# A decoder layer on one core: attention scores and outputs as three float32r products of rounded parts and remainders, with 32 work slots in place of 36

## The chip, the cores and the metric

The kernel runs on one core of one Trainium2 chip. The metric is the device time of one execution in microseconds; the median of the runs is compared. TensorE (PE in the profile) multiplies matrices, with its weight loads listed apart as PEld; VectorE is DVE, ScalarE is ACT, GpSimd is POOL, and SyncE (SP) issues most of the loads. Matrix products are summed in PSUM, in banks of 128 partitions by 512 float32 values. Everything else lives in SBUF.

## The reference

One decoder layer on 512 positions of width 1024, all in float32. It has two halves, a mixer and a feed-forward network (FFN). The mixer projects the normalised input u to queries, keys, values, output gates, forget and input gates (four heads of width 256) and to a convolution group. Queries and keys pass a causal convolution of four taps and SiLU. Per head, with chunks of 128 positions, the reference computes

```python
scores = jnp.einsum("bhtd,bhsd->bhts", q_, k_) * jnp.exp(dmat - m_t[..., None])
num = (w_inter[..., None] * jnp.einsum("bhtd,bhde->bhte", q_, C)
       + jnp.einsum("bhts,bhse->bhte", scores, v_))
den = w_inter * jnp.einsum("bhtd,bhd->bht", q_, n) + jnp.sum(scores, axis=-1)
h = num / jnp.maximum(jnp.abs(den), jnp.exp(-m_t))[..., None]
```

The kernel does this without the chunks' carried state, as one causal attention over all 512 positions: scores times a decay matrix E, then times the values, with two columns of ones behind the values that give the sum of the scores. The heads' outputs are normalised, gated, put beside the convolution group's output (31 taps, layer norm, SiLU), and multiplied by an output matrix. The FFN has an up projection to 2 x 2816, a convolution of three taps, a gated product, and a down projection.

## The kernel before, in words

**Products.** float32 operands are mostly multiplied as three products of float32r values. A tile x is split into a rounded part, hi = x copied by ACT into a float32r tile, and a remainder, lo = x - hi, by POOL or DVE. `mm3` (line 207) then adds hi·hi, hi·lo and lo·hi into one bank. The weights are split by `w_split` (line 185): ACT rounds (line 191), POOL subtracts (line 192). They come through `w_load` from two raw buffers of 1 MB, and a raw buffer is loaded again only when the last remainder has been taken from it. Two products of the attention are not done so: the scores (line 544) and the outputs (line 555) are plain float32 matmuls.

**Attention of one head** (`attention`, line 536) is a generator that is advanced in steps, between which other products are issued. Scores come in four tiles of 512, 384, 256 and 128 columns (causal, one per key chunk), each the sum of two products over the two halves of the head. VectorE multiplies each with its part of E (line 545). Then four output tiles, one per 128 positions, are sums of one to four products of a block of E with 258 columns of values (line 555): ten products a head. ACT takes them out of PSUM (lines 558 to 560), DVE, POOL and ACT work out a factor per position, TensorE transposes (line 586), and ACT and DVE split the result into hh and hl (lines 592, 593). Score, output and transposed tiles share the two banks of `atbank`.

**Order.** TensorE's and SP's instructions are issued in the order of the program. The order on ACT, DVE and POOL is a planner's: it simulates the program, takes the ready instruction of the highest priority (earliest in the program), and gives a tile its buffer when one is free; on the chip each of these engines then follows that order strictly. The taps of the 31-tap convolution (`conv_tile`, line 751: DVE at line 767, ACT and POOL at lines 761 and 763) have their priority lowered by LATER. Two parts (`in_order`) are fixed by hand.

**Loop over heads** (line 836). While head h is in attention, the projections of head h+1 run between its steps: four of q and k (`head_proj`, whose `conv4` at line 498 makes each q or k tile out of PSUM by one ACT, three DVE and one ACT instruction), then four tiles of values and gates (`make_vo`, line 483, where ACT copies the values out at line 494 and gates at line 495). The first steps of the last head's attention stand among the products of the output matrix (`mix_first`, bank mixa; later mixb).

**Buffers.** `slots` holds 36 tiles of 128x512 float32 that nearly everything uses: q and k, E, gates, head outputs, the 32 split tiles hy of heads and convolution group, mg, and in the FFN the split inputs of the down projection (`split_f`, line 1108). `vpool` has two buffers of 128x1032 float32: the values of a head, later a gain row and one pair of `split_f`. `cvs` has four tiles.

**End.** The down projection (line 1179 on, `product`) is one level of a seven-product scheme. It loads weights in groups through the two raw buffers and four `ring` buffers, all on SP's queue. Tiles s34 (11 pairs of slots) and a22 (6 pairs, two of them late) are read back from DRAM and split at lines 1228 and 1229. Ahead of the last product (p4, line 1280), SP's queue holds the load of row g2r into two slots (line 1275) and four loads of x1.

Of the kernel before, what the change touches and what calls it, by code (L numbers as in the profile page):

```python
# [10 lines left out]
F32 = mybir.dt.float32  # L11
F32R = mybir.dt.float32r
BF16 = mybir.dt.bfloat16
AF = mybir.ActivationFunctionType
ALU = mybir.AluOpType
PSUM = bass.MemoryType.PSUM

P = 128
D = 1024
T = 512  # L20
KT = D // P
NT = T // P
H = 4
# [3 lines left out]
CK = 31  # L27
LATER = 100000
EPS = 1e-6
SLOTS = 36  # L30
SIDES = 2
ADAS = 2
SIDE = 5
# [22 lines left out]
def decoder_layer(ctx, tc, w_glu0, x, c, adaT, vecs, w_glu, w_qko, w_v0, w_vo, w_out, w_up, w_down, out):  # L56
# [33 lines left out]
    def slot(name, dt=F32):  # L90
        return slots.tile([P, T], dt, tag="t", name=name)
# [325 lines left out]
        glu_ps[i // 2, i % 2] = ps  # L417
    cspool.__exit__(None, None, None)
    early_pool.__exit__(None, None, None)
    vpool = ctx.enter_context(tc.tile_pool(name="vpool", bufs=2))  # L420
    cvs = ctx.enter_context(tc.tile_pool(name="cvs", bufs=CVS))
    cvpool.append(ctx.enter_context(tc.tile_pool(name="cvpool", bufs=2, space=PSUM)))

# [27 lines left out]


    vs = [None] * H
    gz = const.tile([P, NT, 2 * H], F32, name="gz")
    GB = 2 * H

    def v_tile(h):
        va = vpool.tile([P, 2 * T + 8], F32, tag="vh", name=f"v{h}").rearrange("p (c n) -> p c n", c=NT)

        V.tensor_copy(va[:, :, DH:], ones[:, None, :2].to_broadcast([P, NT, 2]))  # L460
        vs[h] = [va[:, cc, :] for cc in range(NT)]

    def make_v0():

        n = DH + GB
        wv = []
        for q in range(0, KT, 4):
            r = raws.tile([P, 2048], F32, tag="raw", name=f"wv0_{q}")
            nc.sync.dma_start(r[:, : 4 * n], w_v0[q // 4])
            wv += [tuple(w[:, :n] for w in w_split(r[:, i * n : (i + 1) * n], f"wv0_{q + i}")) for i in range(4)]  # L470
        v_tile(0)
        banks = [mmbank(f"v0_{tt}") for tt in range(NT)]
        for tt, ps in enumerate(banks):
            ts = slice(tt * P, (tt + 1) * P)
            for k in range(KT):
                mm3(ps[:, :n], (u[k][0][:, ts], u[k][1][:, ts]), wv[k], k == 0, k == KT - 1)
            V.tensor_tensor(out=gz[:, tt, :], in0=ps[:, DH : DH + GB], in1=vcols("gate_b", 0, GB), op=ALU.add)
            S.activation(vs[0][tt][:, :DH], ps[:, :DH], AF.Copy)

    def part_of(two, tt):  # L480
        return two[tt // 2][:, (tt % 2) * DH : (tt % 2 + 1) * DH]
# [1 line left out]
    def make_vo(h):  # L483

        w = [z for q in range(2) for z in w_load(w_vo[h - 1, q], f"wvo{h}_{q}")]
        v_tile(h)
        gate = [slot(f"so{h}_{i}") for i in range(2)]
        heads[h][3].extend(gate)
        for tt in range(NT):
            ps = mmbank(f"vo{h}_{tt}")  # L490
            ts = slice(tt * P, (tt + 1) * P)
            for k in range(KT):
                mm3(ps, (u[k][0][:, ts], u[k][1][:, ts]), w[k], k == 0, k == KT - 1)
            S.activation(vs[h][tt][:, :DH], ps[:, :DH], AF.Copy)
            S.activation(part_of(gate, tt), ps[:, DH:], AF.Tanh, scale=0.5)
            yield

    def conv4(ps, i, name):

        t = slot(f"{name}c")  # L500
        w = lambda tap: vcol("qk_conv_w", tap * 16 + i)
        S.activation(t, ps, AF.Identity, bias=vcol("qk_conv_b", i), scale=w(3))
        for d in range(1, 4):
            last_e[0] = V.scalar_tensor_tensor(out=t[:, d:], in0=ps[:, : T - d], scalar=w(3 - d), in1=t[:, d:], op0=ALU.mult, op1=ALU.add)
        S.activation(t, t, AF.Silu)
        return t

    hy = [None] * (2 * KT)

# [26 lines left out]
    def attention(h):  # L536
# [3 lines left out]
        for cc in range(NT):  # L540
            n = NS[cc]
            sp = atbank(f"s{h}_{cc}")
            for d in range(2):
                PE.matmul(sp[:, :n], ks[d][:, cc * P : (cc + 1) * P], qs[d][:, cc * P :], start=d == 0, stop=d == 1)  # L544
            last_e[0] = V.scalar_tensor_tensor(out=E[h][cc], in0=sp[:, :n], scalar=DH**-0.5, in1=E[h][cc], op0=ALU.mult, op1=ALU.mult)
            if cc in ((0, 2, 3) if h == 0 else (1, 3)):
                yield
        ssq = small.tile([P, NT], F32, tag="ssq", name=f"ssq{h}")
# [2 lines left out]
        for tt in range(NT):  # L551
            o = atbank(f"o{h}_{tt}")
            for cc in range(tt + 1):
                a = (tt - cc) * P
                PE.matmul(o[:, : DH + 2], E[h][cc][:, a : a + P], vs[h][cc], start=cc == 0, stop=cc == tt)  # L555
            junk = small.tile([P, DH], BF16, tag="junk2", bufs=1, name=f"junko{h}_{tt}")
            hv = hn[tt // 2][:, (tt % 2) * DH : (tt % 2 + 1) * DH]
            S.activation(dm[:, tt : tt + 1], o[:, DH : DH + 1], AF.Abs)
# [56 lines left out]

    PLACE = [(0, 0), (1, 0), (2, 0), (1, 384)]

    def head_tiles(name, dt, three=None):
        three = three or [slots.tile([P, T], dt, tag="t", name=f"{name}{i}") for i in range(3)]
        return [three[s][:, a : a + n] for (s, a), n in zip(PLACE, NS)]  # L620

    E = [None] * H
# [59 lines left out]
    def send_rows(a, n, queue=nc.scalar):  # L682

        ps = mmbank(f"gT{a}") if a == KT else atbank(f"gT{a}")
        PE.transpose(ps[:n, :P], gains[:, a : a + n], ident)
        t = (side if a == 3 * KT else slot)(f"gTs{a}")[:, :P]
        V.tensor_copy(t[:n, :], ps[:n, :P])
        for i in range(n // KT):
            queue.dma_start(rows_d[a // KT + i].rearrange("(j p) -> j p", p=P), t[i * KT : (i + 1) * KT, :])
# [233 lines left out]
    for n in range(10, 2 * KT):  # L923
        mix_first(n)
        if n == 10:
            send_rows(0, KT)
    mg = [slot(f"mg{tt}") for tt in range(NT)]
    x1 = side_parts("x1_0") + side_parts("x1_1")
    x1 = [x1[2 * tt : 2 * tt + 2] for tt in range(NT)]
    wide1 = vpool.tile([P, 2 * T + 8], F32, tag="vh", name="g1r")  # L930
# [189 lines left out]
    for i in range(NF):  # L1120
# [29 lines left out]
        if i % 2:  # L1150
# [6 lines left out]
            if i == NF - 1:  # L1157
                ends = [adas.tile([P, D], F32R, tag="ada", name=f"f{q}{i}") for q in "xy"]
                home = [(z[:, :T], z[:, T:]) for z in ends]
            af.append(split_f(x_, f"fx{i}", i == 1, home[0]))  # L1160
            asum.append(split_f(y_, f"fy{i}", i == 1, home[1]))
            j = i // 2
            nc.scalar.dma_start(spill["s34"][:, j * T : (j + 1) * T], q_)
            nc.scalar.dma_start(spill["a22"][:, j * HT : (j + 1) * HT], r_[:, HT:])
# [200 lines left out]
```

## Time and profile before

| | |
|---|---|
| median of three runs | 771.68 us (770.37 to 772.17) |
| the profiled execution | 771.52 us, of which its span 769.8 us |
| TensorE busy | 758.5 us, 99% of the span |
| DVE, ACT, POOL busy | 573.7, 408.4, 522.7 us |
| TensorE clock granted | 0.998 of full |
| heads' stretch | 157.8 to about 345 us |

Times in the profile are microseconds from the start of the span. A row of a timeline has the start, the duration, the engine and line, and in brackets the idle time before it with what ended that. A row of groups has the number of instructions, their busy time, and the mean nanoseconds of one. The chain of waits follows the execution back from its end, so it lists for each stretch what set the pace. A row of waits has the total time, the number of times, and the longest. Matmul records overlap: their starts, not their durations, give the rate.

### The profile page before, as it was taken

To read this page: it belongs to the slowest core of one execution; us is meant where nothing else is said; L and a number is where in the kernel's file an instruction comes from. 1 tells how busy PE (TensorE), PEld (TensorE's weight loads), DVE (VectorE), ACT (ScalarE), POOL (GpSimd) and SP (SyncE) were. 2 spreads that over 40 slices of the span, in tenths; PEclk is the share of its full clock that TensorE was granted. 3 is DMA by queue.
4 is the path that set the end of the run, shared out by engine and by line. 5 is a ranking of instruction groups with operands and counts; after the bars stand their busy time and mean duration, and the time that the engine had idled before them with its cause. 6 is when DMAs were issued, how large, how long until landed. Compare 5 with 4: busy or idle time off the path is not lost.

```text
span 769.8 us, 10292 instructions
## 1 busy us (share of the span) xinstructions
PE 758.5 (99%) x3562; PEld 630.5 (82%) x3562; DVE 573.7 (75%) x831; ACT 408.4 (53%) x780; POOL 522.7 (68%) x432
## 2 busy tenths in 40 slices
PE   8999999999999999999999999999999999999996
PEld 6788898878788788788888998888888888888885
DVE  5669999979979696476949797675765677654548
ACT  7585438585665645573334554434445246566633
POOL 4789759795494871645611467886978786599943
PEclk9999999999999999999999999999999999999999
DMA  8973214311131250655953655856686584896273
GB/s 317 347 277 126 100 56 140 135 54 56 54 111 55 110 181 38 246 192 164 378 193 135 246 185 196 301 213 232 221 302 220 215 294 145 303 399 239 96 242 141
DMA packets 40137, 147.34 MB, mean 191 GB/s; under 512 B 3826, under 2 KB 5266, under 8 KB 30484
## 3 DMA queue, kind: packets, MB, share of 16 engines
q1 hardware_dynamic: 26372, 94.50, 34.1%
q10 hardware_dynamic: 13712, 52.18, 18.8%
q8 instruction: 28, 0.46, 0.2%
q14 instruction: 25, 0.20, 0.1%
HBM read 126.59 MB, written 20.07 MB: 191 GB/s over the span
## 4 chain that ended last, share of the span: by engine, by line
PE 91%; DMA 2%; DVE 2%; POOL 2%; issue 1%; ACT 1%; DVEq 0%; POOLq 0%; ACTq 0%
PE up L210 31%; PE qko L210 13%; PE dn L210 10%; PE vo L210 9%; PE glu L210 7%; PE mixa L210 6%; PE mixb L210 6%; PE s L544 2%; PE o L555 2%; PE glu L356 2%; PE v L210 1%; DMA p<-spill_t 1%; DMA wglu<-in_w_glu 1%; POOL wglu_0l L192 0%; PE cps L159 0%
## 5 line engine op out<-in xcount | busy, mean ns | idle before, releaser
L767 DVE SCALAR_TENSOR_TENSOR cv<-gt,cvw,cv 128x485 f32<-128x485 f32 (+23 forms) x200 | 137.1, 731 | 2.9 <-ACT cv L755 1.3
L763 POOL TENSOR_TENSOR cs<-cs,cs 128x510 f32<-128x510 f32 (+3 forms) x32 | 42.1, 1318 | 0.1
L210 PE MATMUL up<-u2l,wup_0h 128*128 128x512 f32 (+1 forms) x100 | 36.5, 365 | 0.1
L210 PE MATMUL up<-u2h,wup_0h 128*128 128x512 f32 (+1 forms) x100 | 36.5, 365 | 0.0
L210 PE MATMUL up<-u2h,wup_1024h 128*128 128x512 f32 (+1 forms) x100 | 36.4, 364 | 0.0
L210 PE MATMUL up<-u2h,wup_0l 128*128 128x512 f32 (+1 forms) x100 | 36.4, 364 | 0.0
L210 PE MATMUL up<-u2l,wup_512h 128*128 128x512 f32 (+1 forms) x100 | 36.4, 364 | 0.0
L210 PE MATMUL up<-u2h,wup_512h 128*128 128x512 f32 (+1 forms) x100 | 36.4, 364 | 0.0
L210 PE MATMUL up<-u2h,wup_1536h 128*128 128x512 f32 (+1 forms) x100 | 36.4, 364 | 0.0
L210 PE MATMUL up<-u2l,wup_1536h 128*128 128x512 f32 (+1 forms) x100 | 36.4, 364 | 0.0
L210 PE MATMUL up<-u2h,wup_1536l 128*128 128x512 f32 (+1 forms) x100 | 36.4, 364 | 0.0
L210 PE MATMUL up<-u2h,wup_512l 128*128 128x512 f32 (+1 forms) x100 | 36.4, 364 | 0.0
L210 PE MATMUL up<-u2h,wup_1024l 128*128 128x512 f32 (+1 forms) x100 | 36.4, 364 | 0.0
L210 PE MATMUL up<-u2l,wup_1024h 128*128 128x512 f32 (+1 forms) x100 | 36.3, 363 | 0.0
L176 DVE SCALAR_TENSOR_TENSOR junk<-ada,cb 128x1024 bf16<-128x1024 f32 x20 | 30.1, 1506 | 4.9 <-DMA ada<-in_adaT 4.8
L192 POOL TENSOR_TENSOR wup_0l<-wup,wup_0h 128x512 fp32r<-128x512 f32 x19 | 29.3, 1543 | 4.5 <-ACT wup_0h L191 4.5
L192 POOL TENSOR_TENSOR wup_1024l<-wup,wup_1024h 128x512 fp32r<-128x512 f32 x19 | 25.0, 1318 | 9.4 <-ACT wup_1024h L191 9.4
L192 POOL TENSOR_TENSOR wup_1536l<-wup,wup_1536h 128x512 fp32r<-128x512 f32 x19 | 27.6, 1455 | 4.7 <-ACT wup_1536h L191 4.4
L761 ACT ACTIVATE cs<-gt,cvw 128x511 f32<-128x511 f32 (+4 forms) x40 | 27.2, 712 | 6.3 <-POOL cs L763 3.8
L1099 DVE TENSOR_TENSOR b<-b 128x512 f32<-128x512 f32 x11 | 19.4, 1760 | 11.3 <-POOL b L1098 11.3
L1098 POOL TENSOR_TENSOR b<-b 128x512 f32<-128x512 f32 x11 | 14.2, 1291 | 17.3 <-DVE b L1097 17.3
L336 DVE SCALAR_TENSOR_TENSOR junk<-ada,cps 128x1024 bf16<-128x1024 f32 x16 | 19.5, 1219 | 8.3 <-ACT cb L411 4.6
(1097 smaller groups left out, 2738.5 us busy)
## 6 DMA issues: line engine op xcount, KB each, us to landing
wup<-in_w_up SPq DMA_DIRECT2D x22, 1024.0 KB, 6.0
b<-in_w_down ACTq DMA_DIRECT2D x11, 1024.0 KB, 5.1
spill_t<-b ACTq DMA_DIRECT2D x11, 1024.0 KB, 3.9
ada<-in_adaT ACTq DMA_DIRECT2D x20, 512.0 KB, 4.0
wqko<-in_w_qko SPq DMA_DIRECT2D x9, 1024.0 KB, 4.8
ada<-in_adaT SPq DMA_DIRECT2D x16, 512.0 KB, 7.2
wo<-in_w_out SPq DMA_DIRECT2D x8, 1024.0 KB, 4.8
wvo<-in_w_vo SPq DMA_DIRECT2D x6, 1024.0 KB, 4.8
```

The costliest lines, as they stand in the source:

```text
L176: t = V.scalar_tensor_tensor(out=junk, in0=r, scalar=1.0, in1=cb, op0=ALU.mult, op1=ALU.mult, accum_out=mod[:, i : i + 1])
L192: (eng or G).tensor_tensor(out=lo[:, :n], in0=src, in1=hi[:, :n].bitcast(F32), op=ALU.subtract)
L210: PE.matmul(ps, l, r, start=start and i == 0, stop=stop and i == 2, skip_group_check=again)
L336: V.scalar_tensor_tensor(out=junk, in0=first[k][:, i * D : (i + 1) * D], scalar=1.0, in1=cps, op0=ALU.mult, op1=ALU.mult, accum_out=part[: ...
L356: PE.matmul(ps, blk(wk, i)[a], u[k][b], start=k == 0 and p == 0, stop=k == KT - 1 and p == 1)
L544: PE.matmul(sp[:, :n], ks[d][:, cc * P : (cc + 1) * P], qs[d][:, cc * P :], start=d == 0, stop=d == 1)
L555: PE.matmul(o[:, : DH + 2], E[h][cc][:, a : a + P], vs[h][cc], start=cc == 0, stop=cc == tt)
L761: S.activation(t[:, d:], cvx[j][:, : T - d], AF.Copy, scale=w(CK - 1 - d))
L763: G.tensor_tensor(out=side[:, d:], in0=side[:, d:], in1=t[:, d:], op=ALU.add)
L767: tap = V.scalar_tensor_tensor(out=cp[:, d:], in0=cvx[j][:, : T - d], scalar=w(CK - 1 - d), in1=cp[:, d:], op0=ALU.mult, op1=ALU.add)
L1098: G.tensor_tensor(out=b12, in0=b22, in1=b12, op=ALU.subtract)
L1099: V.tensor_tensor(out=b22, in0=b22, in1=b11, op=ALU.subtract)
```

## The change

- The four q and k tiles of each head are split at the end of `conv4`: ACT rounds, POOL subtracts. Scores use `mm3`, for all four heads: three float32r products where one float32 product stood.
- For heads 0 to 2 (`SPLIT`), each tile of E, once multiplied with its scores, is split too (ACT, POOL), into six more slot tiles Eh and El a head, and the values are split as they leave PSUM (ACT, DVE). Outputs of these heads use `mm3`. Head 3 keeps plain outputs.
- Values take two buffers a head, and `vpool` has four. The columns of ones are written by ACT in place of DVE.
- `slots` shrinks from 36 to 32. The four tiles mg move to two `vpool` buffers, two small rows (gTs) move to `cvs`, and one more pair of `split_f` (i = 3) moves from slots to `vpool`.

```diff
-SLOTS = 36
+SLOTS = 32
...
-    vpool = ctx.enter_context(tc.tile_pool(name="vpool", bufs=2))
+    vpool = ctx.enter_context(tc.tile_pool(name="vpool", bufs=4))
...
+    SPLIT = range(H - 1)
...
     def v_tile(h):
-        va = vpool.tile([P, 2 * T + 8], F32, tag="vh", name=f"v{h}").rearrange("p (c n) -> p c n", c=NT)
-
-        V.tensor_copy(va[:, :, DH:], ones[:, None, :2].to_broadcast([P, NT, 2]))
-        vs[h] = [va[:, cc, :] for cc in range(NT)]
+        both = []
+        for i in range(2 if h in SPLIT else 1):
+            va = vpool.tile([P, 2 * T + 8], F32R if h in SPLIT else F32, tag="vh", name=f"v{h}_{i}").rearrange("p (c n) -> p c n", c=NT)
+            S.activation(va[:, :, DH:], ones[:, None, :2].to_broadcast([P, NT, 2]), AF.Copy, scale=1.0 - i)
+            both.append([va[:, cc, :] for cc in range(NT)])
+        vs[h] = both
+
+    def v_out(h, tt, ps):
+        hi = vs[h][0][tt][:, :DH]
+        S.activation(hi, ps[:, :DH], AF.Copy)
+        if h in SPLIT:
+            V.tensor_tensor(out=vs[h][1][tt][:, :DH], in0=ps[:, :DH], in1=hi.bitcast(F32), op=ALU.subtract)
...
-            S.activation(vs[0][tt][:, :DH], ps[:, :DH], AF.Copy)
+            v_out(0, tt, ps)
...
-            S.activation(vs[h][tt][:, :DH], ps[:, :DH], AF.Copy)
+            v_out(h, tt, ps)
...
         S.activation(t, t, AF.Silu)
-        return t
+        hi, lo = slot(f"{name}h", F32R), slot(f"{name}l", F32R)
+        S.activation(hi, t, AF.Copy)
+        G.tensor_tensor(out=lo, in0=t, in1=hi.bitcast(F32), op=ALU.subtract)
+        return hi, lo
...
-                PE.matmul(sp[:, :n], ks[d][:, cc * P : (cc + 1) * P], qs[d][:, cc * P :], start=d == 0, stop=d == 1)
+                mm3(sp[:, :n], [z[:, cc * P : (cc + 1) * P] for z in ks[d]], [z[:, cc * P :] for z in qs[d]], d == 0, d == 1)
             last_e[0] = V.scalar_tensor_tensor(out=E[h][cc], in0=sp[:, :n], scalar=DH**-0.5, in1=E[h][cc], op0=ALU.mult, op1=ALU.mult)
+            if h in SPLIT:
+                if cc == 0:
+                    Eh, El = head_tiles(f"Eh{h}_", F32R), head_tiles(f"El{h}_", F32R)
+                S.activation(Eh[cc], E[h][cc], AF.Copy)
+                G.tensor_tensor(out=El[cc], in0=E[h][cc], in1=Eh[cc].bitcast(F32), op=ALU.subtract)
...
-                PE.matmul(o[:, : DH + 2], E[h][cc][:, a : a + P], vs[h][cc], start=cc == 0, stop=cc == tt)
+                if h in SPLIT:
+                    mm3(o[:, : DH + 2], (Eh[cc][:, a : a + P], El[cc][:, a : a + P]), (vs[h][0][cc], vs[h][1][cc]), cc == 0, cc == tt)
+                else:
+                    PE.matmul(o[:, : DH + 2], E[h][cc][:, a : a + P], vs[h][0][cc], start=cc == 0, stop=cc == tt)
...
-        t = (side if a == 3 * KT else slot)(f"gTs{a}")[:, :P]
+        t = (side if a == 3 * KT else cvtile)(f"gTs{a}")[:, :P]
...
-    mg = [slot(f"mg{tt}") for tt in range(NT)]
+    wide_mg = [vpool.tile([P, 2 * T + 8], F32, tag="vh", name=f"mg{i}") for i in range(2)]
+    mg = [wide_mg[tt // 2][:, tt % 2 * T : (tt % 2 + 1) * T] for tt in range(NT)]
...
-            af.append(split_f(x_, f"fx{i}", i == 1, home[0]))
-            asum.append(split_f(y_, f"fy{i}", i == 1, home[1]))
+            af.append(split_f(x_, f"fx{i}", i in (1, 3), home[0]))
+            asum.append(split_f(y_, f"fy{i}", i in (1, 3), home[1]))
```

4 lines of the change are left out of this document (2 added, 2 removed).

## The prediction

> **What bounds the kernel now.** I read the totals and the clock first, then the list of what TensorE waited for.
>
> ```profile
> span 769.8 us, 10292 instructions
> PE 758.5 (99%) x3562; PEld 630.5 (82%) x3562; DVE 573.7 (75%) x831; ACT 408.4 (53%) x780; POOL 522.7 (68%) x432
> PEclk9999999999999999999999999999999999999999
> ```
> ```profile
> PE cps L159 <- ACT crow L158: 3.0, 1, 3.0
> PE glu L356 <- ACT uh L397: 1.1, 1, 1.1
> PE s L544 <- DVE hl L593: 0.5, 1, 0.5
> PE xT L252 <- ACT xr L304: 0.3, 1, 0.3
> ```
> TensorE is busy 99% at full clock, and all its waits on others come to 4.9 us, of which one of 0.5 us stands in the stages that change. So time on TensorE is time of the kernel, one for one, as long as the other engines keep up. How near they are is in the three stretches of the heads (busy us of each engine):
>
> ```profile
> 157.80:205.00 47.20, 47.20 (x206) 38.23 (x205) 42.35 (x68) 30.67 (x70) 28.92 (x25) 1.00 0.12 45
> 205.00:258.40 53.40, 53.40 (x238) 43.52 (x237) 47.52 (x71) 33.60 (x73) 39.39 (x32) 1.00 0.23 79
> 258.40:314.90 56.50, 56.05 (x257) 45.49 (x255) 35.73 (x59) 31.56 (x70) 34.24 (x27) 1.00 0.35 128
> ```
> The columns are PE, weight loads, DVE, ACT, POOL. DVE is at 89 to 90% in the first two, POOL at 61 to 74%.
>
> **What the products cost.** From the chain of waits (start, us, pieces); then two rows of TensorE's timeline, then two more of the chain:
>
> ```profile
> 172.58 0.45 PE s L544 x4
> 204.92 3.01 PE s L544 x8
> 219.72 1.31 PE s L544 x8
> 226.52 1.31 PE o L555 x6
> 233.28 1.31 PE o L555 x6
> 240.05 1.74 PE o L555 x8
> ```
> ```profile
> 424.01 0.28 PE L210 MATMUL up<-u2h,wup_512h 128*128 128x256 f32 x1
> 424.13 0.28 PE L210 MATMUL up<-u2l,wup_512h 128*128 128x256 f32 x1
> ```
> ```profile
> 105.92 11.52 PE v L210 x96
> 207.93 5.46 PE qko L210 x24
> ```
> A plain float32 product shows as two matmul records: the last score tile (two products, 128 columns) is four records in 0.45 us, 0.225 a product. A head's scores take 3.01 + 1.31 = 4.32 us, its outputs (ten products of 258 columns) 1.31 + 1.31 + 1.74 = 4.36. A float32r product is one record: 5.46/24 = 0.2275 us at 512 columns, 11.52/96 = 0.120 at 264, and 0.12 from start to start at 256.
>
> After the change a head's scores are 24 products, six at each width: 6 x 0.2275 = 1.37 at 512; at 384 I put 0.174, halfway between 256 and 512, so 1.04; 0.72 at 256. No row shows float32r at 128. It costs between 0.057 (0.2275 in proportion) and the plain float32 product's 0.225; since 256 and 264 both take 0.12, as if something other than columns set it, I take 0.12, so 0.72 again. Sum 3.85, a gain of 0.47 a head and 1.9 over four. (The pair of narrow tiles gets slower, 1.44 for 1.31; the gain is all in the wide pair.) A head's outputs are 30 products at 0.12 = 3.60, a gain of 0.76 and 2.3 over three heads. Together **-4.2 us**. Bounds: at 0.057 for 128 columns and 0.114 for 256 and 258 the gain grows by 1.5 + 0.7, to 6.4; at 0.225 for 128 it shrinks by 24 x 0.105 = 2.5, to 1.7.
>
> [...]
>
> **What the other engines get.** Nearest rows, mean ns ahead of the second bar:
>
> ```profile
> L832 ACT ACTIVATE yh<-gt 128x512 fp32r<-128x512 f32 x8 | 5.0, 619 | 0.3 <-issue 0.3
> L494 ACT ACTIVATE v<-vo 128x256 f32<-128x256 f32 x12 | 4.5, 377 | 10.0 <-PE vo L210 10.0
> L192 POOL TENSOR_TENSOR wqko_0l<-wqko,wqko_0h 128x512 fp32r<-128x512 f32 x9 | 11.7, 1296 | 2.2 <-ACT wqko_0h L191 2.1
> L192 POOL TENSOR_TENSOR wglu_512l<-wglu,wglu_512h 128x256 fp32r<-128x256 f32 x8 | 5.9, 744 | 0.0
> L545 DVE SCALAR_TENSOR_TENSOR E<-s,E 128x256 f32<-128x256 f32 x4 | 1.7, 418 | 3.1 <-PE s L544 3.1
> ```
> Per head, ACT gets four rounded q and k tiles (4 x 0.619) and four of E (0.619, 0.377 at 256, about 0.5 and 0.25 for the widths between and below): 2.5 + 1.75 = 4.2 us. POOL gets the remainders: 4 x 1.296 for q and k, and for E 1.296 + about 1.0 + 0.744 + 0.45 = 3.5, so 8.7. DVE gets four remainders of the values at about 0.418, 1.7, less a small copy of ones that goes to ACT. The fourth head has no split E or values. In the first two stretches of heads ACT had 16.5 and 19.8 us free, POOL 18.3 and 14.0, DVE 4.9 and 5.9; the work fits by sums. What counts is who is late in queues that keep order:
>
> ```profile
> 179.13 1.29 POOL L192 TENSOR_TENSOR wvo_1536l<-wvo,wvo_1536h 128x512 fp32r<-128x512 f32 x1
> 201.71 0.23 POOL L571 TENSOR_SCALAR ssq<-ssq 128x4 f32<-128x4 f32 x1 [17.45 <-ACT so L495]
> 230.01 1.29 POOL L192 TENSOR_TENSOR wvo_1536l<-wvo,wvo_1536h 128x512 fp32r<-128x512 f32 x1 [0.23 <-ACT wvo_1536h L191]
> ```
> ```profile
> 184.63 0.39 PE L210 MATMUL vo<-wvo_1536l,uh 128*128 128x512 f32 x1
> 239.44 0.39 PE L210 MATMUL vo<-wvo_1536l,uh 128*128 128x512 f32 x1
> ```
> ```profile
> 225.82 0.28 DVE L545 SCALAR_TENSOR_TENSOR E<-s,E 128x128 f32<-128x128 f32 x1
> ```
> The last remainder of the value weights of head 1 is ready at 180.42 and used at 184.63: 4.2 us of slack; that of head 2 at 231.30 and 239.44: 8.1. The new remainders stand before it on POOL as far as their data come earlier. The wait of 17.45 us at the head of POOL's queue shows how much room lies unused there, and that order can waste it. Of the 8.7 us of a head, about half falls behind the weights or into such holes, so I cost POOL's and ACT's share at nothing; the cover is the 4.2 us, and if it is gone each us of POOL is a us of TensorE.
>
> The score banks are nearer. The second output tile takes the bank of the narrowest score tile, which DVE frees at 226.10; that product comes at 226.52 + 0.44 = 226.96. DVE now has up to 1.7 us of value remainders in the queue before: a stall of 0 to 0.8 us a head. I take 0.7 for three heads, bounds 0 and 2.4.
>
> **Fewer slots.** In the mixer the splits need up to 32 tiles by my count of lifetimes (hy 32 at its end, with mg now elsewhere). y6 and y7 wait for E of the last head, but are used only by the last pairs of the mix. In the FFN the pair moved to vpool gives back what four slots took. At the end, however, s34 holds 22 slots, a22 12 (4 of them late), ku3 2 and g2r 2. That is 38 for 36 slots before and 32 after, and g2r stands in SP's queue ahead of everything that follows:
>
> ```profile
> SPq L695 <- DVE dn L1219: 17.5, 1, 17.5
> ```
> ```profile
> 735.58 0.89 SPq L695 DMA_DIRECT2D g2r<-row_d  x2
> 738.77 0.37 SPq L1187 DMA_DIRECT2D p<-spill_t  x1
> ```
> ```profile
> 747.31 0.63 ACT L191 ACTIVATE p_1h<-p 128x512 fp32r<-128x512 f32 x1 [10.55 <-DMA p<-spill_t]
> 748.02 1.29 POOL L192 TENSOR_TENSOR p_1l<-p,p_1h 128x512 fp32r<-128x512 f32 x1 [9.18 <-ACT p_1h L191]
> ```
> ```profile
> 737.52 0.39 PE L210 MATMUL dn<-p_2h,s_1024h 128*128 128x512 f32 x1
> 749.99 0.39 PE L210 MATMUL dn<-p_1l,a_0h 128*128 128x512 f32 x1
> ```
> g2r waits 17.5 us for a slot that ku3 gives up; behind it queue four loads of x1 and the weights of the last product (738.77), whose first remainder is done at 749.31 and used at 749.99, 0.7 us of slack. With 32 slots the late a22 tiles and g2r need four more slots, those of s34's first two pieces; the second is free at 737.52 instead of the second g2r load going out 0.5 us after 735.58. That makes the weights 1.4 us later and TensorE wait 0.7. If g2r takes slots ahead of a22 it is 0; I take **0.5**, and 3.4 (two more pieces of p3, 2.7 us) as the upper bound.
>
> **The sum.** 769.8 - 4.2 + 0.7 + 0.5 = 766.8 us of span. The profiled execution lasted 771.52, 1.72 outside its span; so 768.5, and as it lay 0.16 under the median of the runs shown (771.68), **768.6 us**, 0.4% faster. No measurement of this kernel tells less than about 0.2%, 1.5 us, from no change.
>
> **Rivals.**
> - *POOL makes the weights late* (slower). For: it grows from 74% to (39.39 + 8.7)/53.4 = 90% in the second stretch, and it idles behind waits. If all new remainders go before the value weights, heads 1 to 3 stall 8.7 - 4.2 = 4.5 and twice 8.7 - 8.1 = 0.6; ACT's copies before the same weights (three of 512 columns, one of 384) add 2.4. That is 8.1 in place of the 0.7: **776.0**. It decides from the point where over 4.2 us stand ahead in head 1, and is slower than before from 5.3 us of stalls on. Against: the small adds of the convolution (L763) have the lowest priority and give way first.
>
> ```profile
> L192 POOL TENSOR_TENSOR wvo_1024l<-wvo,wvo_1024h 128x512 fp32r<-128x512 f32 x6 | 9.3, 1549 | 2.6 <-ACT wvo_1024h L191 2.6
> ```
>  Some of POOL's adds already take longer, 1549 against 1296 ns. [...] At 1549 ns for each full add POOL's work would be 10.0 us a head instead of 8.7, and the rival's stalls 3 x 1.3 more. In the heads the trace does not bear it out much: wqko_0l has 1296 on average.
> - *The last weights are late* (no change). The slots go to a22 first and g2r gets those of s34's fourth piece: 2.7 more, **771.3**. For: the 17.5 us wait and 0.7 us of slack; against: the late a22 tiles need only four.
> - *Narrow products pay in full* (no change). At 128 columns a float32r product takes what the float32 one takes: 2.5 less gained, **771.1**. Nothing in the trace shows one.
> - *The conversion never runs in three passes* (no change): the values of the last head stay plain, and if the others did too TensorE would gain nothing; against it, mm3 issues three records in 0.68 us everywhere else.
>
> **From these to the numbers.** Forecast 0.54, by itself 766 to 770; POOL 0.23; the last weights 0.14; narrow products 0.08; not converted 0.01. Faster by over 0.2% is the forecast; no change is the two middle rivals, the last and a quarter of POOL's case, 0.29; slower is the rest of it, 0.17. Low end: 768.6 - 2.2 (all products at their lower bound) - 1.2 (no waits) = 765.2, of which I keep 765.8. The high end, 774.0, takes in both middle rivals and the POOL case up to three quarters of its stalls.
>
> **What would show it.** Right: a head's score pieces sum to 3.8 us in the chain and its outputs to 3.6; waits of PE in 157 to 345 stay under 2 us; mix products begin 4 us earlier. g2r goes out 1 to 2 us later against the last product's start. Wrong: waits of PE vo or qko for POOL remainders of weights; PE s waiting for a k remainder; score records of 128 columns over 0.2 us apart; a wait of PE dn before p_1l above 1 us.

## The result: 3.7% slower, and the profile after

The changed kernel takes 800.81 us (median of 4 runs, 800.13 to 801.55) beside 771.92 us before (4 runs, 770.37 to 774.93): a ratio of 1.0369, 95% interval 1.0337 to 1.0402. Forecast were 768.6 us and a range of 765.8 to 774.0. It is 29 us slower, and the range missed it. Ratios here and below leave out the few disturbed executions (one took 903 us), so they can differ a little from the quotient of two medians.

Totals and clock of the kernel after:

```profile
span 799.8 us, 10503 instructions
...
PE 765.2 (96%) x3624; PEld 639.1 (80%) x3624; DVE 575.1 (72%) x839; ACT 427.5 (53%) x815; POOL 555.0 (69%) x460
...
PEclk9999999899997999999999999999999999999999
```

The span grew by 30.0 us. TensorE's idle time went from 769.8 - 758.5 = 11.3 to 799.8 - 765.2 = 34.6 us, which is 23.3 of it. The other 6.7 us are busy time, although the products got shorter: in two slices that hold long waits, the clock row falls to 8 and 7.

What TensorE waited for (us in total, times, longest):

```profile
PE mtok L689 <- DVE Mr L682: 8.2, 1, 8.2
PE o L210 <- ACT hn L579: 7.4, 3, 3.1
PE o L210 <- DVE E L557: 3.3, 2, 3.2
...
PE s L210 <- DVE hl L613: 2.6, 3, 1.8
PE fcum L671 <- DVE g_lf L632: 1.8, 1, 1.8
...
PE dn L210 <- POOL p_1l L192: 0.5, 1, 0.5
```

Before, the longest wait in the heads was 0.5 us. None of the new ones in the heads is for a rounded copy or a remainder that the change added. They are for old work: the scan Mr, the copies hn out of the output banks, the product E, the remainder hl of a head's output, and g_lf. By the first row of each in TensorE's timeline, the same work starts later:

| start of (us) | before | after | later by |
|---|---|---|---|
| running sums fcum | 128.16 | 128.40 | 0.2 |
| scores of head 0 | 157.61 | 169.52 | 11.9 |
| scores of head 1 | 204.76 | 216.93 | 12.2 |
| scores of head 2 | 258.26 | 280.63 | 22.4 |
| scores of head 3 | 314.90 | 343.27 | 28.4 |
| feed-forward stage (up) | 414.83 | 444.02 | 29.2 |

So nearly everything is lost between fcum and the scores of head 3. The same three stretches of the heads, from first score to first score (columns as before: length; busy PE, weight loads, DVE, ACT, POOL; clock, DMA):

```profile
169.70:217.10 47.40, 46.13 (x224) 38.82 (x224) 39.76 (x64) 29.87 (x68) 30.03 (x27) 1.00 0.13 45
217.10:280.80 63.70, 57.22 (x256) 47.60 (x256) 51.60 (x74) 37.84 (x81) 48.31 (x41) 0.92 0.20 69
280.80:343.30 62.50, 56.99 (x274) 47.32 (x273) 34.03 (x56) 34.78 (x74) 39.22 (x32) 0.97 0.32 114
```

No engine is full in these three, where 16.5 of the 29 us are lost: POOL is busy for 117.6 of 173.6 us (68%), DVE for 125.4, ACT for 102.5. In the stretch ahead of them DVE is full, but it was so before without a wait; first the kernel after, from fcum to the end of the wait for Mr, then the kernel before, from fcum to the first scores:

```profile
128.40:156.20 27.80, 19.63 (x85) 15.81 (x85) 26.42 (x43) 16.55 (x28) 24.18 (x20) 0.89 0.32 114
```
```profile
128.16:157.61 29.45, 29.45 (x138) 24.11 (x137) 29.21 (x43) 20.00 (x34) 23.97 (x20) 1.00 0.30 108
```

What differs is what DVE does first: ahead of Mr now stand three taps of k, four value remainders, and twelve more taps of the 31-tap convolution, whose priority is lowered. And of the remainders of q and k the view of their line shows when they ran and, under "who waited for it", nobody:

```profile
L517 POOL TENSOR_TENSOR k_3l<-k_3c,k_3h x4: 1286/1292/1664, 154.4 to 320.1; 128x512 fp32r<-128x512 f32 x4
...
who waited for it (us, times):
busy tenths in 40 slices 0000000201001001000000000000000000000000
```

TensorE waits for none of the new instructions. What is late is old work, which stands at another place in its queue. Where, the timelines show. Before, the scan Mr ran 2.4 us after TensorE's last product for its input had started (140.32):

```profile
142.70 1.20 DVE L662 TENSOR_TENSOR_SCAN Mr<-aT,zero 4x512 f32<-4x512 f32 x1
```

After, that product starts at 142.25, but the scan runs 12.7 us later, right after POOL has started k's second remainder (k_3l), and the copies hn in head 0 stand right behind the rounded copy of k (k_3h), whose remainder POOL starts at 197.44:

```profile
153.74 0.63 ACT L516 ACTIVATE k_3h<-k_3c 128x512 fp32r<-128x512 f32 x1
...
154.44 1.66 POOL L517 TENSOR_TENSOR k_3l<-k_3c,k_3h 128x512 fp32r<-128x512 f32 x1 [2.22 <-DVE cv L787]
...
154.90 1.21 DVE L682 TENSOR_TENSOR_SCAN Mr<-aT,zero 4x512 f32<-4x512 f32 x1
...
196.75 0.62 ACT L516 ACTIVATE k_3h<-k_3c 128x512 fp32r<-128x512 f32 x1
197.27 0.65 ACT L579 ACTIVATE hn<-o 128x256 f32<-128x256 f32 x2
```

Neither Mr nor hn reads k. What they share with k's remainder is the pool: all are tiles of the slots, and in the program k's remainder is written ahead of both. That is the theory that the experiments came to; it took two others to get there.

### The profile page after: what moved, and what is told of

Its sections match the earlier page's. It is cut to its first block, busy times and chain, and to the rows that moved or that the text cites. A ratio compares the mean times of both kernels' runs of the same rounds, so it can differ in the third digit from the quotient of the medians.

```text
span 799.8 us, 10503 instructions
## 1 busy us (share of the span) xinstructions
PE 765.2 (96%) x3624; PEld 639.1 (80%) x3624; DVE 575.1 (72%) x839; ACT 427.5 (53%) x815; POOL 555.0 (69%) x460
## 4 chain that ended last, share of the span: by engine, by line
PE 72%; DVE 12%; ACT 5%; DMA 5%; issue 4%; POOL 1%; SPq 1%; DVEq 0%; ACTq 0%; POOLq 0%
PE up L210 30%; PE dn L210 10%; PE vo L210 8%; PE glu L210 7%; PE qko L210 5%; PE mixa L210 3%; DVE cv L787 3%; PE glu L356 2%; DVE hl L613 1%; DVE junk L176 1%; DMA ada<-in_adaT 1%; PE o L210 1%; PE s L210 1%; DMA xr<-x1d 1%; PE v L210 1%
## 5 line engine op out<-in xcount | busy, mean ns | idle before, releaser
L787 DVE SCALAR_TENSOR_TENSOR cv<-gt,cvw,cv 128x492 f32<-128x492 f32 (+21 forms) x200 | 137.5, 730 | 2.6 <-ACT cv L775 1.3
L1120 DVE TENSOR_TENSOR b<-b 128x512 f32<-128x512 f32 x11 | 19.4, 1762 | 11.3 <-POOL b L1119 11.3
L192 POOL TENSOR_TENSOR wup_512l<-wup,wup_512h 128x512 fp32r<-128x512 f32 x19 | 26.2, 1377 | 0.0
```

Of the source, the lines that this page charges most:

```text
L192: (eng or G).tensor_tensor(out=lo[:, :n], in0=src, in1=hi[:, :n].bitcast(F32), op=ALU.subtract)
L787: tap = V.scalar_tensor_tensor(out=cp[:, d:], in0=cvx[j][:, : T - d], scalar=w(CK - 1 - d), in1=cp[:, d:], op0=ALU.mult, op1=ALU.add)
L1120: V.tensor_tensor(out=b22, in0=b22, in1=b11, op=ALU.subtract)
```

## Experiments

Ratios are to the kernel before, run on the same chip, with a 95% interval. "Place" is the number of an instruction in DVE's queue, counted in the trace without the reads of an accumulator; Mr stands at place 200 before and 218 after. I began with three theories: **order** (the new instructions push old ones back in the fixed queues), **slots** (32 are too few) and **load** (each us of added work on ACT and POOL costs its share).

**Which part: buffers, scores or outputs.** e1 is the kernel before with the buffers of the kernel after alone.

```diff
-SLOTS = 36
+SLOTS = 32
...
-    vpool = ctx.enter_context(tc.tile_pool(name="vpool", bufs=2))
+    vpool = ctx.enter_context(tc.tile_pool(name="vpool", bufs=4))
...
-    mg = [slot(f"mg{tt}") for tt in range(NT)]
+    wide_mg = [vpool.tile([P, 2 * T + 8], F32, tag="vh", name=f"mg{i}") for i in range(2)]
+    mg = [wide_mg[tt // 2][:, tt % 2 * T : (tt % 2 + 1) * T] for tt in range(NT)]
...
```

> The kernel before with the buffers of the kernel after alone: 32 slots, four value buffers, the mixer's rows and two pairs of the feed-forward stage moved out of the slots; nothing is split. Order theory (the loss comes from where the new ACT, POOL and DVE instructions put the old ones in the fixed queues): no loss in the heads, the slots and TensorE's tail cost 0 to 1.5 us, 771.5 to 773.5. Slots theory (the loss comes from planned waits for 32 slots): most of the 29 us is here, 790 to 800.

e2 is the kernel after without the split of E and the values.

```diff
-    SPLIT = range(H - 1)
+    SPLIT = ()
```

> The kernel after with the scores split alone: values, E and outputs stay plain float32, 32 slots. Order theory: the scan Mr stands behind 10 more DVE instructions than before (17 more in the kernel after, where the first scores come 12 us later), so the first scores come about 7 us later, and the later heads lose part of the other 17 us: 777 to 788. Load theory (each us of new work on the busy helpers costs its share): q and k are 2.5 of 4.2 us on ACT and 5.2 of 8.7 us on POOL, so 60% of 29: 789. Slots theory: as the run with the buffers alone.

e3 is the kernel after without the split of q and k.

```diff
-        hi, lo = slot(f"{name}h", F32R), slot(f"{name}l", F32R)
-        S.activation(hi, t, AF.Copy)
-        G.tensor_tensor(out=lo, in0=t, in1=hi.bitcast(F32), op=ALU.subtract)
-        return hi, lo
+        return t
...
-                mm3(sp[:, :n], [z[:, cc * P : (cc + 1) * P] for z in ks[d]], [z[:, cc * P :] for z in qs[d]], d == 0, d == 1)
+                PE.matmul(sp[:, :n], ks[d][:, cc * P : (cc + 1) * P], qs[d][:, cc * P :], start=d == 0, stop=d == 1)
```

> The kernel after with the outputs split alone: q, k and scores stay plain float32, 32 slots. Order theory: the scan Mr stands where it stood before, so the first scores come no later than before (within 2 us); what is lost comes in the later heads: 771 to 783. Load theory: 40% of 29 us, 783, spread over the heads. Slots theory: as the run with the buffers alone.

Measured: buffers 772.98 us, ratio 1.0012 (0.9998 to 1.0026); scores 799.75 us, 1.0340 (1.0303 to 1.0378); outputs 775.12 us, 1.0028 (1.0014 to 1.0042). The scores alone make nearly the whole loss. Of TensorE's waits in e2:

```profile
PE mtok L689 <- DVE Mr L682: 8.5, 1, 8.5
PE o L575 <- ACT hn L579: 5.3, 2, 3.3
```

Three things follow. The buffers cost about what the forecast gave to the slots, 0.5 us, and can't be told from no cost. The load theory falls: 60% of the added work makes over 90% of the loss, and the other 40% next to nothing. The order theory is right in where (Mr is at place 212 with the scores, at 201 with the outputs) but much too low in how much.

**Mr itself.** In e4, the kernel after, the block of Mr is written ahead of the projection that it stood behind.

```diff
     head_proj(0, 2)
-
-    head_proj(0, 3)
     aps = atbank("aT")
     for tt in range(NT):
         PE.transpose(aps[:H, tt * P : (tt + 1) * P], ga[:, tt, :], ident)
     Mr = slot("Mr")[:H, :]
...
     V.tensor_tensor(out=Mhl[LO : LO + H, :], in0=Mr, in1=Mhl[:H, :].bitcast(F32), op=ALU.subtract)
+    head_proj(0, 3)
     head_proj(0, 4)
```

> The kernel after with one block of lines moved up: the transposes aT, the scan Mr and its split are written ahead of the projection of k's second half instead of behind it, so that the scan stands 9 places earlier on DVE; same instructions, same work. Order theory: the wait of TensorE for Mr (8.2 us) shrinks by about 6 us, and the time by 5 to 8 us, 793 to 796. Slots and load theories: nothing is taken away, the delay shows up at the next stage: 799 to 802.

Measured: 798.36 us, 1.0326 (1.0276 to 1.0376). Mr stands at place 210 and TensorE's wait for it shrank by 5.8 us (8.2 to 2.4), as the order theory had it; the time went down by only 2.4 us by the medians (800.81 to 798.36) and 3.3 by the ratios, whose intervals overlap, where 5 to 8 were expected. Part of the rest is given back further on: TensorE waits 3.1 us for hn in head 0 in place of 1.3. That Mr moved at all by being written earlier, ahead of the second half of k, and that it had come up right behind k's remainder, led to the **turn** theory: tiles of one pool take their slots in the written order.

The next two part it from the number of slots. e5 is e2 with 36 slots and the other buffers of the kernel before; e6 is e5 with Mr in memory of its own.

```diff
-SLOTS = 32
+SLOTS = 36
...
```

> The scores split alone once more, with the buffers of the kernel before: 36 slots, two value buffers. Slots theory (too few slots): most of the 27 us of the run with 32 slots comes back, 772 to 780. Turn theory (tiles of one pool get their slots in the order in which they are written in the program, so a tile written behind k's remainder cannot start before POOL has reached that remainder, however many slots are free): nothing comes back, 797 to 801, and TensorE waits for the scan Mr as before, 8 us.

```diff
-SLOTS = 36
+SLOTS = 35
-    Mr = slot("Mr")[:H, :]
+    Mr = const.tile([P, T], F32, name="Mr")[:H, :]
```

> The scores split alone, 35 slots, and the scan Mr in memory of its own instead of a slot; no other line differs from the run with 36 slots. Turn theory: the scan no longer waits for its turn behind k's remainder; it stands 13 places earlier on DVE, TensorE's wait for it (8 us) is gone, the first scores come 8 to 12 us earlier, and what is lost in the later heads (hn, E and gates still take turns) stays: 787 to 793. Order by load (the added work of ACT and POOL delays whatever comes): the wait moves to the next stage, 797 to 801.

Measured: e5 794.07 us, 1.0307 (1.0264 to 1.0349); e6 798.41 us, 1.0352 (1.0327 to 1.0377). The 36 slots bring nothing that can be told apart from 32 (the intervals overlap; the time is 3 us under the 797 to 801 expected), and Mr stands at the same place, 212, so it is not their number. With Mr in memory of its own it stands at place 199, runs 14 us ahead of k's remainder, TensorE no longer waits for it, and the first scores start at 157.64 (157.61 before). From DVE's and POOL's rows of e6:

```profile
144.59 1.20 DVE L682 TENSOR_TENSOR_SCAN Mr<-aT,zero 4x512 f32<-4x512 f32 x1
...
158.57 1.71 POOL L517 TENSOR_TENSOR k_3l<-k_3c,k_3h 128x512 fp32r<-128x512 f32 x1
```

And yet the time is no lower, which the expectation missed. The gain went to the tiles next in line: TensorE waits 1.4 us more for k's remainder, 1.8 more for E, and for hn, where it was 5.0 us in e5:

```profile
PE o L575 <- ACT hn L579: 12.5, 3, 7.1
```

**All turns.** If it is the turns, no tile may stand behind a late one. Two ways: write the splits elsewhere in the program, or leave them and give them their slots early. e7 is the kernel after with the splits written at the head's first scores.

```diff
-        hi, lo = slot(f"{name}h", F32R), slot(f"{name}l", F32R)
-        S.activation(hi, t, AF.Copy)
-        G.tensor_tensor(out=lo, in0=t, in1=hi.bitcast(F32), op=ALU.subtract)
-        return hi, lo
+        return t, name
+
+    def split_qk(h):
+
+        _, qs, ks, _ = heads[h]
+        for two in (qs, ks):
+            for d, (t, name) in enumerate(two):
+                hi, lo = slot(f"{name}h", F32R), slot(f"{name}l", F32R)
+                S.activation(hi, t, AF.Copy)
+                G.tensor_tensor(out=lo, in0=t, in1=hi.bitcast(F32), op=ALU.subtract)
+                two[d] = hi, lo
...
         _, qs, ks, so = heads[h]
+        split_qk(h)
```

> The kernel after with one edit: the rounded parts and remainders of q and k are written in the program at the head's first scores instead of right behind each convolution. Same instructions, same tiles, 32 slots. Turn theory: Mr, E, the gates and hn take their slots ahead of the remainders, as in the kernel before; the first scores come within 3 us of the kernel before and the waits of TensorE in 128 to 345 us fall from some 22 us to under 6: 768 to 775. Load theory: the work is the same, 795 to 801.

e8 is the kernel after with two one-column copies in each convolution.

```diff
+        hi, lo = slot(f"{name}h", F32R), slot(f"{name}l", F32R)
         S.activation(t, ps, AF.Identity, bias=vcol("qk_conv_b", i), scale=w(3))
+        S.activation(hi[:, :1], ps[:, :1], AF.Copy)
+        S.activation(lo[:, :1], ps[:, :1], AF.Copy)
...
-        hi, lo = slot(f"{name}h", F32R), slot(f"{name}l", F32R)
         S.activation(hi, t, AF.Copy)
```

> The kernel after with 32 added instructions: right behind a convolution's first instruction ACT copies one column into the tile of the rounded part and one into that of the remainder, so both take their slots at once instead of at the end of the convolution; every other line stays where it is. Turn theory: nothing waits behind a remainder's turn any more; Mr stands on DVE where it stood before, TensorE's waits for Mr and for hn (15.6 us together) go below 4 us, and the time falls to 768 to 778. Load theory: more work than after on ACT (32 x about 0.2 us), 799 to 806. If only order at Mr mattered, 790.

e9 is e7 with the calls in the middle.

```diff
-        split_qk(h)
...
     head_proj(0, 4)
+    split_qk(0)
...
+        split_qk(h + 1)
         make_E(h + 1)
```

> The kernel after with the rounded parts and remainders of q and k written in the middle: of head 0 behind the projection that follows Mr, of the others behind hn and ahead of the next E. In the run where they were written at the scores, the waits for Mr and hn were gone and 27 us of waits for the remainders themselves stood in their place. Turn theory with a lead time: both go, 767 to 776. If the remainders' own work is what costs (POOL and ACT too full to have them ready in time), TensorE waits for k's remainders at the scores again, 785 or more.

Measured: e7 813.63 us, 1.0543 (1.0503 to 1.0582); e8 776.63 us, 1.0029 (1.0002 to 1.0057), with three executions at 771 us, the profiled one (770.95) among them, and five at 774 to 778, a spread that stays unexplained; e9 772.40 us, 1.0002 (0.9987 to 1.0017).

e7 missed, and tells why. The waits for Mr and hn are gone, as the theory said, but written last, the splits come last, and now TensorE waits for them at the scores, some 27 us:

```profile
PE s L210 <- POOL k_2l L524: 13.1, 4, 4.3
PE s L210 <- ACT k_2h L523: 9.0, 3, 3.9
PE s L210 <- POOL k_3l L524: 4.4, 3, 2.8
```

e8 settles it. It has all the instructions of the kernel after, in the same written order, and 32 more, and by the ratios (1.0369 and 1.0029) it is 26 us faster. Nor is it less loaded: from fcum (127.3) to its first scores (156.8) POOL is busy for all 29.5 us and DVE for 29.2, and TensorE waits for neither. Those 32 do nothing but write one column into the new tiles, which are asked for when the convolution starts instead of at its end. ACT's rows in head 0: hn no longer waits behind the rounded copy, but runs 6 us ahead of it.

```profile
179.72 0.15 ACT L513 ACTIVATE k_3h<-qko 128x1 fp32r<-128x1 f32 x1
179.87 0.40 ACT L581 ACTIVATE hn<-o 128x256 f32<-128x256 f32 x1
...
186.01 0.62 ACT L518 ACTIVATE k_3h<-k_3c 128x512 fp32r<-128x512 f32 x1
```

e9 reaches the same by moving the splits to where they are early enough to be ready and late enough that nothing urgent stands behind them. In e7, e8 and e9 alike Mr is back at place 201. So the cause is shown: in this kernel the tiles of the slots take their slots in the order of the program. The planner therefore put the tiles written behind the split of k (Mr and hn by the rows above; E's and the gates by the same argument, with no row shown) behind the first writes of that split, which come last in the chain of taps, Silu, rounded copy and remainder, and the queues keep what the planner fixed: in the kernel after, dm read hn's bank at 191.23, ACT then stood idle for 3.75 us up to 195.86, and hn came only at 197.27, behind k_3h. The rule itself stands in no trace; what the runs show is that Mr and hn move when the turn of the split moves, and that nothing else has to change for it. Whether the turn goes by the line that asks for a tile or by its first write stays open, since e8 moved both together.

**What the products alone are worth.** e10 is e2 with the rounded tile written by Silu itself, its slot taken early as in e8, and no remainder: it leaves out what makes the three products exact, and is for its time alone.

```diff
+        hi = slot(f"{name}h", F32R)
...
+        S.activation(hi[:, :1], ps[:, :1], AF.Copy)
...
-        S.activation(t, t, AF.Silu)
-        hi, lo = slot(f"{name}h", F32R), slot(f"{name}l", F32R)
-        S.activation(hi, t, AF.Copy)
-        G.tensor_tensor(out=lo, in0=t, in1=hi.bitcast(F32), op=ALU.subtract)
-        return hi, lo
+        S.activation(hi, t, AF.Silu)
+        return hi, hi
```

> Scores alone as in the second run, with the three products but without the helpers' work: Silu writes the rounded tile itself (its slot taken at once), and all three products read it; rounded copies, remainders and their accuracy are left out. What the products alone are worth: my prediction 0.47 us a head less, 1.9 us in all, so 770 to 772 beside 772.5 with the same buffers. If TensorE's own work were the cause (slower products, another clock), 790 or more.

Measured: 771.99 us, 0.9995 (0.9980 to 1.0009), where the expectation was 770 to 772. By the trace the gain is there. From fcum to the second half of the mix (first row of each in TensorE's timeline), before:

```profile
128.16 0.29 PE L651 MATMUL fcum<-g_lf,tri 128*128 128x16 f32 x2
...
369.33 0.39 PE L210 MATMUL mixb<-wo_0h,hh 128*128 128x512 f32 x1
```

and in e10:

```profile
128.79 0.29 PE L670 MATMUL fcum<-g_lf,tri 128*128 128x16 f32 x2
...
368.01 0.39 PE L210 MATMUL mixb<-wo_0h,hh 128*128 128x512 f32 x1
```

241.17 and 239.22 us: 1.95 less, where 1.9 was forecast for the scores. But fcum starts 0.6 later in e10, and behind the mix TensorE waits 0.7 for DVE's u2l and 0.8 for the last weights. A gain of this size is not to be told from no change in the whole.

**Where the rest of the gain stays.** With the order mended (e9) the kernel only equals the kernel before, so four runs looked at what is left. e11 is e9 with g2r in a value buffer, e12 is e11 with outputs split in heads 1 and 2 alone, and e13 and e14 are e12 and e11 with the four rounded tiles written ahead of the four remainders.

```diff
-    g2r = row(3, lambda n: [slot(f"{n}r{hf}") for hf in range(2)], "g2", nc.sync)
+    wide2 = vpool.tile([P, 2 * T + 8], F32, tag="vh", name="g2r")
+    g2r = row(3, lambda n: [wide2[:, :T], wide2[:, T : 2 * T]], "g2", nc.sync)
```
```diff
-    SPLIT = range(H - 1)
+    SPLIT = range(1, H - 1)
```
```diff
-                hi, lo = slot(f"{name}h", F32R), slot(f"{name}l", F32R)
+                hi = slot(f"{name}h", F32R)
                 S.activation(hi, t, AF.Copy)
+                both.append((two, d, t, hi, name))
+        for two, d, t, hi, name in both:
+            lo = slot(f"{name}l", F32R)
...
```

> The run with the splits written in the middle, and the two rows g2r of the last stage in one value buffer, free by then, instead of two of the 32 slots. That run was 4.0 us faster than the kernel before between the first sums fcum and the feed-forward stage, and lost it to a wait of TensorE for g_lf ahead of fcum (1.7 us) and to 0.8 us more in the last products. If g2r's wait for a slot is what costs in the last products, they come back to the 105.1 us of the kernel before: 771.2, 0.1 to 0.2% under before. If the order of the slots elsewhere costs there, no change from 772.4.

> As the run before this one, and values and E of head 0 left plain float32: only heads 1 and 2 take three products for their outputs. DVE has no value remainders (4 x 0.4 us) ahead of g_lf. If those four delay g_lf, TensorE's wait ahead of fcum is gone and 1.7 us come back, less the 0.8 us that head 0's outputs gain: about 770.3, 0.2% under the kernel before. If the wait has another cause, 772.

> The run with outputs split in heads 1 and 2, with one edit: the four rounded tiles of q and k are written first and the four remainders after them, so that a rounded tile takes its slot without waiting for the remainder ahead of it. There TensorE waited 2.6 us at the first scores for k's second remainder, which stood on POOL behind a weight and an addition. Turn theory: that wait goes, the stretch from fcum to the feed-forward stage gets 2 to 3 us shorter, and the time is 770 to 771, 0.2% under the kernel before, with the products' gain of heads 1 to 3 left standing. If POOL's and ACT's work is the limit there, no change from 773.4.

> The same edit in the run with all three heads' outputs split and g2r in a value buffer (771.4). No wait for a remainder stood there, so turn theory expects little, 770.5 to 772; the 1.6 us of TensorE's wait for g_lf ahead of fcum stay, since DVE's four value remainders of head 0 stay.

Measured: e11 771.42 us, 0.9994 (0.9981 to 1.0008); e12 773.42 us, 1.0032 (1.0010 to 1.0053); e13 771.77 us, 0.9984 (0.9963 to 1.0004); e14 773.38 us, 1.0011 (0.9995 to 1.0027). None is told from the kernel before but e12, which is slower; e12 and e14 came out above every time that was expected of them, e13 between its two. Each wait that goes lets a small one show elsewhere: e9 waits 1.7 for g_lf ahead of fcum, e12 only 0.4, but 2.6 for k's remainder at the first scores; e13 still 1.5 and 0.7 there, in place of the none expected; e14 1.8 for g_lf and 1.8 for E ahead of a transpose. That the last products lose to g2r's slot holds: from their first start to their last end e11 needs 105.3 us (e9 105.9, before 105.1). That DVE's four value remainders of head 0 delay g_lf is likely but not shown: of the eight kernels that have them seven wait 1.6 to 1.8 us there, and those without wait 0 to 0.5, but e8 has all four and waits 0.5. No version beats both kernels measurably.

## Why the prediction was wrong, step by step

**What bounds the kernel**: right, with the condition that it named itself: time on TensorE is time of the kernel "as long as the other engines keep up". They did not. (The terms of the sum come to 768.7, not 768.6, which decides nothing.)

**The products**: right. Pieces of the chain in the kernel after, a last output tile, two wide score tiles and two narrow ones, and then two 128-column products in TensorE's timeline:

```profile
204.50 1.44 PE o L210 x12
217.10 2.42 PE s L210 x12
348.75 1.33 PE s L210 x12
```
```profile
232.08 0.27 PE L210 MATMUL s<-q_0h,k_2l 128*128 128x128 f32 x1
232.19 0.27 PE L210 MATMUL s<-q_1h,k_3h 128*128 128x128 f32 x1
```

A head's scores take 2.42 + 1.33 = 3.75 us (forecast 3.85), an output product 1.44/12 = 0.12 (0.12). At 128 columns it is 0.11 (0.12 taken, with bounds of 0.057 and 0.225), so the rival "narrow products in full" is out. For all seven splits (scores of four heads, outputs of three) the row in e9 is

```profile
367.73 0.39 PE L210 MATMUL mixb<-wo_0h,hh 128*128 128x512 f32 x1
```

With fcum at 129.82 there (its row is in the last section) the stretch takes 237.91 us, 3.3 less than before, with a wait of 0.55 for k_3l and one of 0.34 for ysq in it, and one of 0.45 for hl in the kernel before. Without the waits of both it is 3.7 less, where 4.2 was forecast.

**What the other engines get**: this is the step that failed. Its sizes were right: ACT's rounded copies took 0.62 us and POOL's remainders 1.29 to 1.54 on average. So was its sentence that what counts is who is late in queues that keep order. But it then asked this only of two things, the value weights and the score banks, and concluded "so I cost POOL's and ACT's share at nothing". It never asked at which place the old instructions would stand once the new tiles were written ahead of them. In its place the runs showed a cost of some 26 us (kernel after against e8): TensorE waits for Mr, hn and E, whose instructions now stand late in their queues, and its clock is slower at those waits (granted 0.984 over the span, 0.999 in e8). No row of before could have been added up to it; what could be read was that q, k, Mr, E, the gates and hn all come from one pool, and that the new tiles, written between them, are first written at the end of a chain of 3 taps, Silu and copy.

**Fewer slots**: the count of tiles was asked, not their order. As a count it held: the buffers alone cost 0.4 us by the medians of one chip (772.98 to 772.54) and 0.9 by the ratio, neither told from nothing, and TensorE's wait for p_1l in the kernel after is 0.5 us, where 0.5 was taken.

**Score banks**: forecast 0.7 us for three heads; the kernel after shows 3.3 us of "PE o <- DVE E", outside the bounds of 0 to 2.4. With the order mended, in e9, there is none, so the term was not the wrong one; it was priced for a queue that stays as it was.

**Rivals.** POOL makes the weights late: the sign was right, the mechanism not. No wait of TensorE in the heads names a value weight, and POOL was 68% busy in the three stretches. It is the near relative that came true, a queue held up by where something stands, at over three times the price (29 us beside 8.1). The last weights are late: out, TensorE's wait for p_1l is 0.5 us, where this rival had 2.7 more. Conversion never runs: out, by the rows above.

**What would show it**: the list of what would prove the forecast wrong named waits for remainders and weights. The waits that came in the heads were for neither; the line "waits of PE in 157 to 345 stay under 2 us" was the one that told: they came to 13.3 us, with the 8.2 for Mr just ahead of them.

## What to carry to other kernels

When an edit puts new tiles into a shared pool, ask not only how many there are but when each is first written, and which tiles written behind it are urgent: here the scan Mr, which reads nothing of k, ran 12 us late for the turn of k's remainder. Give a late tile an early first write (e8) or a later place in the program (e9), but not the last: e7 lost 42 us by coming too late, where the change had lost 29 by coming too early. Memory of its own for one urgent tile only moved the wait to the next (e6); a pool of their own for the late tiles was not tried. And free time on an engine, added up, did not tell here what stood late in its queue: POOL was 68% busy in the three stretches of the heads.

## What the runs showed of the chip

In the kernel after one wait of TensorE cost about twice its length. After 1.76 us without work ahead of fcum the products start 0.43 us apart for a while, instead of 0.23:

```profile
128.40 0.40 PE L671 MATMUL fcum<-g_lf,tri 128*128 128x16 f32 x2 [1.76 <-DVE g_lf L632]
...
130.28 0.63 PE L210 MATMUL qko<-uh,wqko_0l 128*128 128x512 f32 x1
130.71 0.63 PE L210 MATMUL qko<-uh,wqko_0h 128*128 128x512 f32 x1
131.14 0.63 PE L210 MATMUL qko<-ul,wqko_0h 128*128 128x512 f32 x1
...
133.28 0.39 PE L210 MATMUL qko<-ul,wqko_0h 128*128 128x512 f32 x1
133.52 0.39 PE L210 MATMUL qko<-uh,wqko_0l 128*128 128x512 f32 x1
```

Eight such products cost 8 x 0.2 = 1.6 us more. Over the whole kernel this makes nearly all of the difference in busy time between two kernels with the same 3624 matmul records, 765.2 us after (granted clock 0.984) and 755.0 in e8 (0.999): in the kernel after the clock is at half in five stretches ahead of the end, 23.91 us, with 19.55 us of busy TensorE, half of which is 9.8. The totals of e8:

```profile
PE 755.0 (98%) x3624; PEld 632.1 (82%) x3624; DVE 577.2 (75%) x839; ACT 425.6 (55%) x847; POOL 560.8 (73%) x460
```

So 10 of the 30 us are not the waits but the slower clock at and behind them. (The products themselves gain: 758.5 us busy before, 755.0 in e8. With the 10.2 that makes the 6.7 more of the kernel after.) It does not follow every wait: in e9 the wait at the same place was as long, and the clock stayed up.

```profile
129.82 0.40 PE L678 MATMUL fcum<-g_lf,tri 128*128 128x16 f32 x2 [1.74 <-DVE g_lf L639]
...
131.05 0.39 PE L210 MATMUL qko<-ul,wqko_0h 128*128 128x512 f32 x1
131.28 0.40 PE L210 MATMUL qko<-uh,wqko_0l 128*128 128x512 f32 x1
```

What differs is where the wait falls. In the trace of the kernel after the clock changes only at whole multiples of 3.413 us from its first change, between full and half: to half at 129.36, 153.25, 242.00, 252.24 and 313.68 us, back at 132.78, 160.08, 245.41, 259.07 and 317.10, and to half at 798.37, when TensorE has no more work. One stretch between two such multiples holds the whole wait (busy TensorE 1.65 of 3.41 us, then half clock in the next); in e9 the wait is divided over the two stretches shown, 2.57 and 2.51 us busy, and the clock stays full:

```profile
125.94:129.35 3.41, 1.65 (x13) 1.19 (x11) 3.41 (x5) 3.08 (x5) 3.41 (x3) 1.00 0.11 12
129.37:132.76 3.39, 3.39 (x9) 2.71 (x9) 3.39 (x8) 2.44 (x5) 2.77 (x4) 0.50 0.75 288
```
```profile
125.51:128.92 3.41, 2.57 (x12) 1.80 (x10) 3.41 (x5) 3.41 (x7) 3.41 (x4) 1.00 0.40 171
128.92:132.33 3.41, 2.51 (x15) 2.25 (x16) 3.41 (x5) 2.77 (x5) 3.30 (x3) 1.00 0.40 118
```

Up to 760 us, nine such stretches of the kernel after are at full clock and have over 1 us without TensorE work. Those with 1.76, 2.15, 2.61, 2.81 and 3.41 us were followed by half clock; those with 1.02, 1.20, 1.59 and 1.84 were not.
